# Down product of an encoder block: one more pair of k tiles by seven products in the second half of columns

## The chip, the cores and the metric

The kernel runs on one core of a Trainium2 chip. The metric is the device time of one execution in microseconds (us); the kernel before takes 1113.47 us, the median of 3 runs (1113.41 to 1113.65). Engines are named as in the profile: PE (TensorE, the matmuls), PEld (its weight loads), DVE (VectorE), ACT (ScalarE), POOL (GpSimd) and SP (SyncE, here only an issuer of DMAs).

## The reference, cut to what matters

One encoder block over 256 positions of width 2048: a mixer, then a gated conv-MLP, then a per-layer embedding gate. The change lies in the MLP, whose inner width is 5632:

```python
def conv_glu(hn, w_up, conv_w, conv_b, w_down):
    up = hn @ w_up
    gate, val = jnp.split(up, 2, axis=-1)
    gate = dwconv_centred(gate, conv_w, conv_b)
    return (jax.nn.gelu(gate, approximate=True) * val) @ w_down
```

All of it is float32. The last line's product, (256 x 5632) by (5632 x 2048), is called the down product here; `hn @ w_up` is up, and the gate product of the embedding that follows is (256 x 2048) by (2048 x 2048).

## The kernel before

**Arithmetic.** PE multiplies numbers of the shortened type fp32r, so each float32 operand is split in a high part (a cast on ACT, L153 for weights, L945 for activations) and a low part (a subtraction on DVE, L154 and L946). One product becomes three: high by high, high by low, low by high.

**The down product** runs in two halves of 1024 columns, `dn0` and `dn1` (`sublayer`, L835, and `token_major`, L306). In each half the 44 k tiles of 128 rows are taken as 22 pairs, u = 0 to 21; pair u has the tiles k = 2u and 2u + 1, and tiles in traces bear the number k: `dn122` is the second half's pair u = 11. A pair is done in one of two ways.

- *Ordinary*: the pair's weights (128 x 2048 values, 1 MB, tile `dn1r`) are loaded and split in two parts of 1024 (`dn_0`, `dn_1`); PE does 24 matmuls of 512 columns (2 k tiles, 2 halves of the tokens, 2 halves of the columns, 3 products).
- *By seven products* (`seven_products`, L256): the pair is read as a 2 x 2 matrix of blocks by a 2 x 2 matrix of blocks, and Strassen's scheme in Winograd's form needs 7 block products in place of 8, so 21 matmuls of 512. It needs sums of blocks on both sides. On the weight side the sums s1 to s4 are four DVE additions of 128 x 512 (`add_blocks`, L250); they are made while up runs and are kept in DRAM, so that a pair loads two blocks of the weights themselves (tile `r`, 768 KB) and the page with the sums (tile `t`, 1 MB). These are split in four parts, named a (512 wide), b, d and c (1024 wide each), in this order. On the activation side the sums are 128 x 512 values with their low parts (tile `hd`, 512 KB): for some pairs (`dn_stored`) they are made while up runs and are stored in `hsum` (L955 to L965), and POOL's queue loads them (L1073); for the others DVE and ACT make them on the spot (L803 to L808). The partial products that belong to several outputs are collected in four accumulators (`dns`, `dn0s`, `dn1s`) over all the pairs so treated, and `combine` (L284) adds them up once per half.

`dn_fast` (L920) lists the pairs by seven products: 17 in the first half, 15 in the second. Ordinary in the second half are u = 0, 1, 6, 10, 17, 20 and 21. At u = 11 of the second half the job `first` loads and splits a first piece of the gate product's weights (`gtf`, 1 MB).

**Up** runs in 176 pieces of 16 matmuls. Between the pieces other jobs are set out by a hand-written list, `jobs_at`: for each pair in `which` (the pairs of the down and the gate product by seven products, 37 of them, two of which come last) a `fetch` of the weights at piece n, and at piece n + 3 an `add` (the four additions) and a `store` to DRAM on POOL's queue (tile `dns`); the last two stay in SBUF. In up the order within ACT, DVE and SP is the order of the program (`in_order`, L200). In down a scheduler at build time decides the order on each engine; on the chip each engine takes its instructions in that fixed order.

**Buffers** that decide when something can start: high parts and low parts of weights have 5 buffers each, raw weights 3 (so a load is issued when DVE has made the low part b of the pair that was loaded three loads before), activation parts `hs` 2, `mid` tiles (among them `hd`) 3, and pages of 128 x 2048 (weight sums `t`, hidden activations, the gate weights) 13 in all. Loads of `r` and `t` are issued on SP's queue, loads of `hd` on POOL's.

Of the kernel before, what the change touches and what calls it, by code (L numbers as in the profile page):

```python
# [53 lines left out]
def build(nc, a, out):  # L54
# [6 lines left out]
    with tile.TileContext(nc) as tc, \  # L61
# [165 lines left out]
        def block_sums(name, w, c0, k, held):  # L227


            pg = []  # L230

            def fetch():
                r = page(f"{name}b{c0}_{k}")
                pg.append(r)
                load(r, w[c0 // 1024, k // 2])

            def add():
                add_blocks(pg[0])
                if held:
                    sums_[name, c0, k] = pg[0], True  # L240

            def store():
                if not held:
                    t = dp.tile([P, 2048], F32, tag=f"{name}s{c0}_{k}", bufs=1, name=f"{name}s{c0}_{k}")
                    nc.gpsimd.dma_start(t, pg[0])  # L245
                    sums_[name, c0, k] = t, False

            return fetch, add, store
# [668 lines left out]
            h_kept.append(dp.tile([P, D], F32, tag=f"h{t}", bufs=1, name=f"h_kept{t}"))  # L917
        pl_kept = dp.tile([P, D], F32, tag="pl", bufs=1, name="pl_kept")

        dn_fast, gt_fast = ((2, 3, 4, 5, 7, 8, 9, 10, 11, 12, 13, 14, 15, 16, 17, 18, 19), (2, 3, 4, 5, 7, 8, 9, 11, 12, 13, 14, 15, 16, 18, 19)), ((4, 5, 6), (1, 2))  # L920

        dn_stored = (2, 3, 5, 7, 8, 10, 11, 13, 14, 16, 17, 18, 19)
        gt_ks = list(range(NK)), [0, 1, 8, 9, 10, 11, 2, 3, 4, 5, 6, 7, 12, 13, 14, 15]
# [6 lines left out]
        jobs_at[6].append(lambda: load(pl_kept, pl[0]))  # L930
        for i, w_ in enumerate(which[2:] + which[:2]):
            fetch, add, store = block_sums(*w_, i >= len(which) - 2)
            n = 46 * i // 10 + 4
            jobs_at[n].append(fetch)
            jobs_at[n + 3].extend((add, store))
        hid, kept = [], {}
# [87 lines left out]
        with in_order():  # L1024
            for _ in range(5):
                next_part()
            for n in range(NPIECES):
                s, v, i = blocks[n // 4]
# [235 lines left out]
```

## Time and profile before

| | |
|---|---|
| median of the runs | 1113.47 us |
| the profiled execution | 1113.6 us, its span 1111.8 us |
| granted PE clock, mean | 0.998 of full |
| up, from the first of its matmuls to the last | about 292 to 786 us of the span |
| down, first half and second half | about 786 to 896 us and 896 to 1007 us |

The span is what the profiler sees of one execution on the core; some 1.8 us of the measured time lie outside it. A view by windows gives the busy time of each engine in a stretch; a timeline lists instructions with their start and duration; the chain of waits goes back from the last instruction to what released it. Busy times on DVE and ACT are of single instructions that overlap at their ends: how fast an engine gets through a row of them is read from start to start.

### The profile page before, as it was taken

To read this page: it belongs to the slowest core of one execution; us is meant where nothing else is said; L and a number is where in the kernel's file an instruction comes from. 1 tells how busy PE (TensorE), PEld (TensorE's weight loads), DVE (VectorE), ACT (ScalarE), POOL (GpSimd) and SP (SyncE) were. 2 spreads that over 40 slices of the span, in tenths; PEclk is the share of its full clock that TensorE was granted. 3 is DMA by queue.
4 is the path that set the end of the run, shared out by engine and by line. 5 is a ranking of instruction groups with operands and counts; after the bars stand their busy time and mean duration, and the time that the engine had idled before them with its cause. 6 is when DMAs were issued, how large, how long until landed. Compare 5 with 4: busy or idle time off the path is not lost.

```text
span 1111.8 us, 16068 instructions
## 1 busy us (share of the span) xinstructions
PE 1102.2 (99%) x5964; PEld 951.3 (86%) x5964; DVE 959.5 (86%) x1339; ACT 724.0 (65%) x1057; POOL 75.7 (7%) x140
## 2 busy tenths in 40 slices
PE   9999999999999999999999999999999999999997
PEld 9999988888888888888888888888888888888876
DVE  6568997899868998888888888898899999999995
ACT  6958763555775564665655646657579877877673
POOL 0200000100100000000000000000000000021001
PEclk9999999999999999999999999999999999999999
DMA  9853356454589999999899999899999899996763
GB/s 363 323 195 140 114 188 267 152 190 171 194 357 401 401 372 385 350 377 374 341 378 374 360 383 366 351 392 390 353 384 386 333 344 399 413 394 226 274 237 105
DMA packets 54943, 347.29 MB, mean 312 GB/s; under 512 B 6096, under 2 KB 6992, under 8 KB 20176
## 3 DMA queue, kind: packets, MB, share of 16 engines
q1 hardware_dynamic: 44064, 289.53, 67.1%
q0 software_dynamic: 10368, 56.10, 13.4%
q8 instruction: 47, 0.77, 0.3%
q10 hardware_dynamic: 432, 0.62, 0.2%
q14 instruction: 32, 0.26, 0.1%
HBM read 297.48 MB, written 48.76 MB: 311 GB/s over the span
## 4 chain that ended last, share of the span: by engine, by line
PE 92%; ACT 3%; DMA 2%; DVE 1%; issue 1%; POOL 0%; SPq 0%; POOLq 0%; ACTq 0%
PE ga L90 22%; PE va L90 22%; PE dna L90 12%; PE woa L90 7%; PE xbc L90 5%; PE gt L90 5%; PE z L90 4%; PE dns L90 4%; PE dn0s L90 2%; PE dn1s L90 2%; DMA dtur<-w_dtu 2%; PE ple L90 1%; DMA x<-x 1%; PE yd L90 1%; PE pw L90 1%
## 5 line engine op out<-in xcount | busy, mean ns | idle before, releaser
L90 PE MATMUL ga<-wox,ug_0h 128*128 128x512 f32 x352 | 125.5, 395 | 0.0
L90 PE MATMUL ga<-wox,ug_1h 128*128 128x512 f32 x352 | 125.1, 394 | 0.0
L90 PE MATMUL va<-wox,uv_1h 128*128 128x512 f32 x352 | 124.8, 393 | 0.0
L90 PE MATMUL va<-wox,uv_0h 128*128 128x512 f32 x352 | 124.8, 393 | 0.0
L90 PE MATMUL ga<-wox,ug_1l 128*128 128x256 f32 x352 | 99.1, 282 | 0.0
L90 PE MATMUL va<-wox,uv_1l 128*128 128x256 f32 x352 | 99.1, 281 | 0.0
L90 PE MATMUL va<-wox,uv_0l 128*128 128x256 f32 x352 | 99.1, 281 | 0.0
L90 PE MATMUL ga<-wox,ug_0l 128*128 128x256 f32 x352 | 99.0, 281 | 0.0
L254 DVE TENSOR_TENSOR dnb<-dnb 128x512 f32<-128x512 f32 x128 | 88.3, 690 | 3.1
L90 PEld LDWEIGHTS va<-wox,uv_0h 128*128 128x128 f32 x352 | 66.1, 188 | 15.0
L90 PEld LDWEIGHTS va<-wox,uv_1h 128*128 128x128 f32 x352 | 66.1, 188 | 15.0
L90 PEld LDWEIGHTS ga<-wox,ug_1h 128*128 128x128 f32 x352 | 66.1, 188 | 15.0
L90 PEld LDWEIGHTS ga<-wox,ug_0h 128*128 128x128 f32 x352 | 66.1, 188 | 14.8
L90 PEld LDWEIGHTS ga<-wox,ug_0l 128*128 128x128 f32 x352 | 66.2, 188 | 0.1
L90 PEld LDWEIGHTS ga<-wox,ug_1l 128*128 128x128 f32 x352 | 66.2, 188 | 0.0
L90 PEld LDWEIGHTS va<-wox,uv_1l 128*128 128x128 f32 x352 | 66.2, 188 | 0.0
L90 PEld LDWEIGHTS va<-wox,uv_0l 128*128 128x128 f32 x352 | 66.2, 188 | 0.0
L945 ACT CAST hs<-hid 128x512 fp32r<-128x512 f32 x44 | 27.1, 620 | 17.7 <-PE dna L90 17.6
L245 POOL DMA_DIRECT2D dns<-dnb x30 | 16.2, 540 | 309.9 <-DVE dnb L254 299.9
L946 DVE TENSOR_TENSOR hs<-hid,hs 128x512 fp32r<-128x512 f32 x44 | 30.0, 688 | 3.4 <-ACT hs L945 3.4
L807 ACT CAST he<-he 128x512 fp32r<-128x512 f32 x13 | 8.1, 621 | 36.6 <-DVE he L806 36.6
L90 PE MATMUL dna<-dn_0h,hs 128*128 128x512 f32 x96 | 31.3, 394 | 0.0
(2247 smaller groups left out, 3235.5 us busy)
## 6 DMA issues: line engine op xcount, KB each, us to landing
dnb<-w_down SPq DMA_DIRECT2D x32, 1024.0 KB, 10.0
dns<-dnb POOLq DMA_DIRECT2D x30, 1024.0 KB, 6.7
hd<-hsum POOLq DMA_DIRECT2D x24, 512.0 KB, 8.5
zr<-w_z SPq DMA_DIRECT2D x8, 1024.0 KB, 5.0
dtur<-w_dtu SPq DMA_DIRECT2D x14, 528.0 KB, 8.2
wo0r<-w_out_ SPq DMA_DIRECT2D x7, 1024.0 KB, 4.8
dn1r<-w_down SPq DMA_DIRECT2D x7, 1024.0 KB, 9.2
hsum<-he POOLq DMA_DIRECT2D x13, 512.0 KB, 7.1
```

The lines of the kernel that those rows point to most:

```text
L90: last["pe"] = ins(nc.tensor.matmul(o, lhsT, rhs, start=start, stop=stop, skip_group_check=True))
L245: nc.gpsimd.dma_start(t, pg[0])
L254: nc.vector.tensor_add(v[:, i], v[:, i], v[:, j])
L807: nc.scalar.copy(o[:, :512], s[:, :512])
L945: nc.scalar.copy(t[:, :512], hid_part(k))
L946: nc.vector.tensor_sub(t[:, 512:], hid_part(k), t[:, :512].bitcast(F32))
```

## The change

The pair u = 10 (k tiles 20 and 21) of the second half of columns is moved from the ordinary pairs to those by seven products. Its activation sums are already made and stored for the first half (10 is in `dn_stored`), and its weight sums join the list of blocks in up, which then has 38 entries; the factor that spreads the entries over the pieces of up goes from 46 to 45 tenths.

```diff
-        dn_fast, gt_fast = ((2, 3, 4, 5, 7, 8, 9, 10, 11, 12, 13, 14, 15, 16, 17, 18, 19), (2, 3, 4, 5, 7, 8, 9, 11, 12, 13, 14, 15, 16, 18, 19)), ((4, 5, 6), (1, 2))
+        dn_fast, gt_fast = ((2, 3, 4, 5, 7, 8, 9, 10, 11, 12, 13, 14, 15, 16, 17, 18, 19), (2, 3, 4, 5, 7, 8, 9, 10, 11, 12, 13, 14, 15, 16, 18, 19)), ((4, 5, 6), (1, 2))
...
         for i, w_ in enumerate(which[2:] + which[:2]):
             fetch, add, store = block_sums(*w_, i >= len(which) - 2)
-            n = 46 * i // 10 + 4
+            n = 45 * i // 10 + 4
             jobs_at[n].append(fetch)
             jobs_at[n + 3].extend((add, store))
```

In the built program the second half then has 21 matmuls for this pair in place of 24, four weight splits on ACT and on DVE in place of two, a load of 768 KB and one of 1 MB on SP's queue in place of one of 1 MB, and one more load of 512 KB on POOL's queue; up has four more additions on DVE, one more 1 MB load and one more 1 MB store.

## The prediction

> **What bounds the kernel now.** I read the page first, then the chain of waits, then windows, then the timelines of DVE, PE, ACT and POOL around the pair that changes.
>
> ```profile
> span 1111.8 us, 16068 instructions
> PE 1102.2 (99%) x5964; PEld 951.3 (86%) x5964; DVE 959.5 (86%) x1339; ACT 724.0 (65%) x1057; POOL 75.7 (7%) x140
> PE 92%; ACT 3%; DMA 2%; DVE 1%; issue 1%; POOL 0%; SPq 0%; POOLq 0%; ACTq 0%
> ...
> 763.69 22.33 PE va L90 x128
> ...
> 500.00:550.00 50.00, 50.00 (x289) 43.90 (x288) 42.36 (x57) 31.03 (x47) 2.66 (x5) 1.00 0.92 357
> 896.00:1006.00 110.00, 110.00 (x478) 89.45 (x477) 104.64 (x128) 84.20 (x107) 12.01 (x11) 1.00 0.96 385
> 946.00:976.00 30.00, 30.00 (x132) 24.40 (x131) 29.93 (x38) 25.25 (x33) 2.15 (x4) 1.00 1.01 409
> ```
>
> The first rows (page) give PE as the bound of the whole: 99% busy, 92% of the chain that ended last. A window's columns are PE, PEld, DVE, ACT and POOL busy, granted PE clock, DMA share, GB/s. The three windows are a stretch of up, all of the second down half, and its 30 us from pair u = 11 on. In up DVE has some 15% to spare. In the last window nothing has: PE 30.00 of 30, DVE 29.93 of 30, the DMA engines at a share of 1.01. A cut of PE's work is worth its time there only if the other two still deliver in time. So the share of the span is the wrong view for this change; the question is by how much DVE and the DMAs are ahead of PE at u = 11 and after.
>
> **What PE saves.** The chain of waits shows PE's pieces in order (start, duration, engine, tile, count):
>
> ```profile
> 937.64 2.07 PE dna L90 x9
> 942.47 2.08 PE dna L90 x9
> 946.63 5.55 PE dna L90 x24
> 952.87 2.07 PE dna L90 x9
> ```
>
> From 942.47 back to 937.64 is 4.83 us: one pair by seven products, 21 matmuls. The ordinary pair u = 10 is the 24 matmuls from 946.63: 5.55 us, 0.231 us each. Three fewer save 3 x 0.231 = 0.69 us, all of it on the path. That is the whole gain that the change can have: 0.06% of the span.
>
> **What DVE gains in work.** The timeline of DVE around the pair (start, duration, engine, line, operation, tiles, count; idle time before and its releaser in brackets):
>
> ```profile
> 940.82 1.23 DVE L154 TENSOR_TENSOR dn118dl<-dn118t,dn118dh 128x1024 fp32r<-128x1024 f32 x1 [0.74 <-ACT dn118dh L153]
> ...
> 943.10 1.22 DVE L154 TENSOR_TENSOR dn_0l<-dn1r,dn_0h 128x1024 fp32r<-128x1024 f32 x1
> 944.24 1.22 DVE L154 TENSOR_TENSOR dn_1l<-dn1r,dn_1h 128x1024 fp32r<-128x1024 f32 x1
> ...
> 945.97 2.35 DVE L154 TENSOR_TENSOR gtfl<-gtf,gtfh 128x1024 fp32r<-128x1024 f32 x2
> ...
> 948.85 0.68 DVE L154 TENSOR_TENSOR dn122al<-dn122r,dn122ah 128x512 fp32r<-128x512 f32 x1
> 949.45 1.22 DVE L154 TENSOR_TENSOR dn122bl<-dn122r,dn122bh 128x1024 fp32r<-128x1024 f32 x1
> ...
> 952.24 1.22 DVE L154 TENSOR_TENSOR dn122dl<-dn122t,dn122dh 128x1024 fp32r<-128x1024 f32 x1
> ...
> 954.51 0.69 DVE L946 TENSOR_TENSOR hs<-hid,hs 128x512 fp32r<-128x512 f32 x1
> 955.12 0.69 DVE L154 TENSOR_TENSOR dn124al<-dn124r,dn124ah 128x512 fp32r<-128x512 f32 x1
> 955.72 1.22 DVE L154 TENSOR_TENSOR dn124bl<-dn124r,dn124bh 128x1024 fp32r<-128x1024 f32 x1
> 956.85 1.22 DVE L154 TENSOR_TENSOR dn124dl<-dn124t,dn124dh 128x1024 fp32r<-128x1024 f32 x1
> ...
> 985.12 1.22 DVE L154 TENSOR_TENSOR dn136cl<-dn136t,dn136ch 128x1024 fp32r<-128x1024 f32 x1 [0.52 <-ACT dn136ch L153]
> ```
>
> DVE waits before 940.82, and the next wait that the timeline marks is the one before 985.12: between them it runs back to back through u = 10 to 17. From start to start a split of 1024 takes 1.14 us (943.10 to 944.24) and one of 512 takes 0.60 (948.85 to 949.45). The ordinary pair's two splits cost 2 x 1.14 = 2.28. By seven products they are four: 0.60 + 3 x 1.14 = 4.02. DVE gets 1.74 us more, in a row without a hole, so everything that it delivers until 985 comes 1.74 us later. Ordinary pairs are the places where DVE draws ahead of PE (2.28 and the 0.60 of an L946 against 5.55 us), and u = 10 stands just before `gtf`, 2.35 us that belong to no pair. The edit takes away the rest that paid for it.
>
> **How far DVE is ahead.** PE's first uses of those parts, from its timeline:
>
> ```profile
> 952.02 0.39 PE L90 MATMUL dns<-dn122ah,hs 128*128 128x512 f32 x1
> 954.32 0.39 PE L90 MATMUL dna<-dn122dl,hs 128*128 128x512 f32 x1
> 957.78 0.40 PE L90 MATMUL dna<-dn124bl,hs 128*128 128x512 f32 x1
> 958.93 0.39 PE L90 MATMUL dna<-dn124dl,hs 128*128 128x512 f32 x1
> ```
>
> `dn122dl` is done at 952.24 + 1.22 = 953.46 and used at 954.32: 0.86 us ahead. `dn124bl` is done at 956.94, used at 957.78: 0.84. `dn124dl`: 958.07 against 958.93, 0.86. After the change DVE is 1.74 later, while PE asks 0.69 earlier.
>
> Step by step, with the order of the built program. For u = 11 it puts an L946 (0.60) ahead of `dn122dl`, and makes the matmul that needs `dn122dl` the 14th of the pair in place of its 11th. `dn122dl` is done at 953.46 + 1.74 + 0.60 = 955.80. PE would begin the pair at 952.02 - 0.69 = 951.33 and reach the 14th at 951.33 + 13 x 0.231 = 954.33. PE waits 1.47 us. It is then 1.47 - 0.69 = 0.78 later than before. `dn124bl` comes at 956.94 + 1.74 = 958.68 and is asked for at 957.78 + 0.78 = 958.56: 0.12 more. `dn124dl` comes at 959.81 and is asked for at 959.83: nothing. The short cut agrees: 1.74 of work less the smallest lead of 0.84 is 0.90. Behind the waiting matmul stand all later ones, since PE takes them in order; what is late next is nothing, because u = 17 (ordinary, not changed) again gives DVE time, and the idle before 985.12 shows that it then waits for others. What PE lost by then is not made up.
>
> **What the DMAs gain in work.** ACT's wait for a load, POOL's loads of activation sums, and the times to landing in the second half:
>
> ```profile
> 949.21 1.06 ACT L153 CAST dn122dh<-dn122t 128x1024 fp32r<-128x1024 f32 x1 [0.47 <-DMA dn122t<-dns]
> ...
> 937.24 0.54 POOL L1073 DMA_DIRECT2D hd<-hsum  x1 [14.69 <-DVE dn116dl L154]
> 946.93 0.54 POOL L1073 DMA_DIRECT2D hd<-hsum  x1 [9.15 <-PE dn1s L90]
> ...
> dn1r<-w_down SPq DMA_DIRECT2D x5, 1024.0 KB, 9.2
> hd<-hsum POOLq DMA_DIRECT2D x9, 512.0 KB, 8.4
> ...
> dn118t<-dns SPq DMA_DIRECT2D x1, 1024.0 KB, 10.9
> ...
> dn118r<-w_down SPq DMA_DIRECT2D x1, 768.0 KB, 8.8
> ```
>
> In place of one load like `dn1r` come one like `dn118r`, one like `dn118t` and one `hd`: 768 + 1024 + 512 - 1024 = 1280 KB more, 1.31 MB. The engines are full at 409 GB/s (window above), so all that lands behind it lands up to 1.31 / 0.409 = 3.2 us later. `dn122t` landed at 949.2, when ACT began; 3.2 later is 952.4, the cast `dn122dh` ends at 953.5, and DVE, busy with its own queue, wants it only at 955.80 - 1.22 = 954.58. So 1.1 us of cover is left, and the DMAs add nothing beyond DVE's delay. Bounds: 0, or the whole 3.2 in place of the 0.90 if that cover and the later ones fail. I take 0, nearest to the row with the wait of 0.47. On POOL's queue the new load takes the place of 937.24 and the next one moves to about 942, when u = 8 frees a `mid` buffer; landing 8.4 later, at 950.4, it is still ahead of its first use by the 7th matmul, 951.33 + 6 x 0.231 = 952.7.
>
> The Trainium skill, SBUF — State Buffer, section Summary: rules for kernel authors, tells one to reckon transfers between HBM and SBUF at about 358 GB/s. By that page the extra load would be an estimate of 3.7 us in place of 3.2; the trace differs, with 409 GB/s in the window, and the measurement decides.
>
> **ACT and up.** ACT gets two casts more there; it is busy 84.20 of 110 us in the second half, so its own waits for PE cover them. In up, one block more: four additions, one load, one store.
>
> ```profile
> L254 DVE TENSOR_TENSOR dnb<-dnb 128x512 f32<-128x512 f32 x128 | 88.3, 690 | 3.1
> ...
> 775.16 1.22 DVE L154 TENSOR_TENSOR uv_1l<-uv101r,uv_1h 128x1024 fp32r<-128x1024 f32 x1
> ...
> 783.31 0.28 PE L90 MATMUL va<-wox,uv_1l 128*128 128x256 f32 x1
> ```
>
> 4 x 0.69 = 2.8 us of DVE, spread with the others (45 tenths of a piece for 46). The last part of up is made at 776.38 and used at 783.31, 6.9 us ahead; PE's stretches of 128 matmuls have no hole (22.33 above). I take 0; with the cover gone it is 2.8.
>
> **The sum.** -0.69 (PE) + 1.47 + 0.12 (waits for DVE) + 0 (DMA) + 0 (ACT, up) = +0.90 on the profiled execution's 1113.6 us (span 1111.8 and 1.8 around it): 1114.5. The median shown is 0.1 lower, 1113.47, so I say 1114.4.
>
> **The rivals.**
> - *The saving arrives.* DVE is in time after all, for instance because its row before 985 can close up, and 0.69 comes off: 1112.8. For it: PE's three matmuls are certain. Against: leads of 0.84 to 0.86 against 1.74 of new work with no idle to take it.
> - *The DMAs become the bound (slower).* From u = 10 to 16 the stretch is paced by bytes and ends 3.2 later: 1113.6 + 3.2 = 1116.8. It decides once loads come over 1.1 us later than reckoned at `dn122t`. For it: share 1.01, and ACT already waits for `dn122t`. Against: DVE's own delay of 1.74 covers half. By the Trainium skill's rate above it would be 1117.3, an estimate.
> - *Up loses its cover.* The denser additions make PE wait there, up to 2.8 on top: 1117.3. Against: the lead of 6.9.
> - *The change does not do what it says.* Excluded by the built program: 21 matmuls stand in place of 24.
>
> **How the numbers follow.** Forecast 60% (its own range 1113.6 to 1116.0: PE waits from half to twice the reckoned 1.59), DMA-bound 23%, saving arrives 9%, up 6%, anything else 2%. A measurement of this kernel can tell about 0.2% from no change, 2.2 us: below 1111.2 is faster, above 1115.7 slower. Faster 0.02: no gain beyond 0.69 is to be had. Slower: 0.23 + 0.06 and 0.03 from the forecast's upper end, 0.32. Within: 0.66. The range leaves out the last part of either end: 1112.7 to 1117.0.
>
> **What would show it.** Right: PE waits of 1 to 2 us in all at u = 11 and 12 of the second half, for DVE's low parts; u = 10 in 4.83 us; up unchanged at 22.33 per 128; the end of down some 0.9 later. Wrong: no PE wait there, waits for a DMA at u = 11 to 16, or a hole in up's matmuls.

## The result and the profile after

| | before | after |
|---|---|---|
| median, same chip (22 runs each) | 1113.55 us (1113.03 to 1114.44) | 1115.12 us (1114.01 to 1117.05) |
| the profiled execution | 1113.6 us, span 1111.8 | 1116.33 us, span 1114.5 |

The ratio is 1.0015, with a 95% interval of 1.0009 to 1.0021: 1.6 us slower. The executions of after lie twice as far apart as those of before. The profiled one, 2.7 us slower than that of before, is among the slower, so its waits say where time is lost, and not how much the median execution loses at each place.

From the page of after (span; busy time of each engine; the chain that ended last by engine):

```profile
span 1114.5 us, 16077 instructions
...
PE 1102.9 (99%) x5961; PEld 950.5 (85%) x5961; DVE 964.2 (87%) x1345; ACT 725.3 (65%) x1059; POOL 72.1 (6%) x142
...
PE 90%; ACT 3%; DMA 2%; DVE 2%; issue 1%; POOL 0%; SPq 0%; POOLq 0%; ACTq 0%
```

By windows (a stretch of up, the second half of down, its 30 us from 946 on; columns as before):

```profile
500.00:550.00 50.00, 50.00 (x288) 43.90 (x287) 42.45 (x57) 31.78 (x48) 2.12 (x4) 1.00 0.98 373
896.00:1006.00 110.00, 108.25 (x466) 86.56 (x465) 104.32 (x129) 84.77 (x107) 7.18 (x12) 1.00 0.98 394
946.00:976.00 30.00, 29.44 (x125) 22.77 (x124) 29.93 (x36) 25.42 (x32) 2.15 (x4) 1.00 1.02 418
```

From the chain of waits, up's piece that answers to the one of before:

```profile
763.91 22.33 PE va L90 x128
```

The page's 99% for PE says nothing; the window does. PE, which was busy for the whole of the second half before, now lacks 1.75 us of its 110. Up's 128 matmuls take 22.33 us as before. The view of PE's waits in down's second half, which has no row before, has three:

```profile
PE dna L90 <- ACT hs L945: 1.2, 1, 1.2
PE dna L90 <- DVE dn122dl L154: 0.4, 1, 0.4
PE dns L90 <- ACT dn122ch L153: 0.2, 1, 0.2
```

PE's timeline at u = 10 and 11 (start, duration, line, tiles; idle time before and its releaser in brackets):

```profile
946.68 0.39 PE L90 MATMUL dns<-dn120ah,hs 128*128 128x512 f32 x1
...
951.51 0.40 PE L90 MATMUL dns<-dn122ah,hs 128*128 128x512 f32 x1
...
953.37 0.39 PE L90 MATMUL dna<-dn122bh,hd 128*128 128x512 f32 x1
953.68 0.50 PE L90 MATMUL dna<-dn122dh,hs 128*128 128x512 f32 x1
954.02 0.40 PE L90 MATMUL dn1s<-dn122dh,hd 128*128 128x512 f32 x1
954.62 0.50 PE L90 MATMUL dns<-dn122ch,hd 128*128 128x512 f32 x1 [0.21 <-ACT dn122ch L153]
954.97 0.39 PE L90 MATMUL dn1s<-dn122ch,hd 128*128 128x512 f32 x1
955.71 0.50 PE L90 MATMUL dna<-dn122dl,hs 128*128 128x512 f32 x1 [0.35 <-DVE dn122dl L154]
956.05 0.40 PE L90 MATMUL dna<-dn122dh,hs 128*128 128x512 f32 x1
```

The pair u = 10 takes 951.51 - 946.68 = 4.83 us: the three matmuls are saved. Starts that follow each other by more than 0.231 us are time lost, and that is more than the brackets say, since PE's step behind a wait is longer too (0.34 us from 955.71 to 956.05). From 953.37 to 954.97 four steps take 1.60 in place of 0.92, 0.68 lost to the high parts `dn122dh` and `dn122ch`; from there to 956.05 two take 1.08 in place of 0.46, 0.62 lost to the low part `dn122dl`. With 0.10 more at u = 12 the first wait is 1.40 us. The two rows that feed these matmuls, on ACT and on DVE:

```profile
952.57 1.05 ACT L153 CAST dn122dh<-dn122t 128x1024 fp32r<-128x1024 f32 x1 [1.36 <-DMA dn122t<-dns]
954.44 1.22 DVE L154 TENSOR_TENSOR dn122dl<-dn122t,dn122dh 128x1024 fp32r<-128x1024 f32 x1
```

ACT waited for the load of `dn122t`, so the high parts are late by the load; the low part, done at 955.66, is late by DVE's row. The second wait stands where the prediction has none, at the ordinary pair u = 17. PE's timeline first, then ACT's, then SP's queue with the issue of the load that ACT waited for (first in the kernel before, then in the change), and that load's row in the change's view of DMA issues (its last number is the time to landing):

```profile
981.77 0.39 PE L90 MATMUL dn1s<-dn132ch,hd 128*128 128x512 f32 x1
983.35 0.72 PE L90 MATMUL dna<-dn_0h,hs 128*128 128x512 f32 x2 [1.19 <-ACT hs L945]
```

```profile
977.02 1.05 ACT L153 CAST dn132dh<-dn132t 128x1024 fp32r<-128x1024 f32 x1 [1.39 <-DMA dn132t<-dns]
977.97 1.04 ACT L153 CAST dn132ch<-dn132t 128x1024 fp32r<-128x1024 f32 x1
980.78 1.05 ACT L153 CAST dn_0h<-dn1r 128x1024 fp32r<-128x1024 f32 x1 [1.77 <-PE dna L90]
981.74 1.04 ACT L153 CAST dn_1h<-dn1r 128x1024 fp32r<-128x1024 f32 x1
982.69 1.14 ACT L945 CAST hs<-hid 128x512 fp32r<-128x512 f32 x2
```

```profile
966.19 0.33 SPq L120 DMA_DIRECT2D dn1r<-w_down  x1
...
967.78 0.33 SPq L120 DMA_DIRECT2D dn1r<-w_down  x1
```

```profile
dn1r<-w_down SPq DMA_DIRECT2D x1, 1024.0 KB, 12.9
```

PE loses 983.35 - 981.77 - 0.23 = 1.35 us, and the profile names the activation cast `hs`. That cast is only the last of a row on ACT: it stands behind `dn_0h` and `dn_1h`, and `dn_0h` starts at 980.78. For that cast the profile names PE, but the load was issued at 967.78 and took 12.9: it landed at 980.7. The cause of PE's wait is thus a late load, two steps behind the name in the bracket. Before, it was issued 1.59 us earlier and took 9.6: it landed at 975.8, 4.9 us earlier. So 1.6 us of its lateness is later issue and 3.3 a longer way. The issue hangs on DVE: it follows the low part `dn128bl`, which frees a raw buffer and is done at 967.75 in place of 966.16. In all the profiled execution has -0.69 + 1.40 + 1.45 (0.10 for the longer step behind the wait at u = 17 included) = 2.16 us more at the end of this half; its start into down was 0.2 later from up on. That is more than the 1.57 us between the medians; how these divide between the two waits is not shown.

### The profile page after: what moved, and what is told of

The parts are those of the page before. It is cut to its first block, busy times and chain, and to the rows that moved or that the text cites. A ratio compares the mean times of both kernels' runs of the same rounds, so it can differ in the third digit from the quotient of the medians.

```text
span 1114.5 us, 16077 instructions
## 1 busy us (share of the span) xinstructions
PE 1102.9 (99%) x5961; PEld 950.5 (85%) x5961; DVE 964.2 (87%) x1345; ACT 725.3 (65%) x1059; POOL 72.1 (6%) x142
## 4 chain that ended last, share of the span: by engine, by line
PE 90%; ACT 3%; DMA 2%; DVE 2%; issue 1%; POOL 0%; SPq 0%; POOLq 0%; ACTq 0%
PE ga L90 22%; PE va L90 22%; PE dna L90 11%; PE woa L90 7%; PE xbc L90 5%; PE gt L90 5%; PE z L90 4%; PE dns L90 4%; PE dn0s L90 2%; DMA dtur<-w_dtu 2%; PE dn1s L90 2%; PE ple L90 1%; DMA x<-x 1%; PE yd L90 1%; PE pw L90 1%
## 5 line engine op out<-in xcount | busy, mean ns | idle before, releaser
L254 DVE TENSOR_TENSOR dnb<-dnb 128x512 f32<-128x512 f32 x132 | 91.1, 690 | 3.2
L946 DVE TENSOR_TENSOR hs<-hid,hs 128x512 fp32r<-128x512 f32 x44 | 29.9, 685 | 2.3 <-ACT hs L945 2.3
L90 PE MATMUL dna<-dn_0h,hs 128*128 128x512 f32 x88 | 29.0, 394 | 1.2 <-ACT hs L945 1.2
```

The lines of the kernel that those rows point to most:

```text
L90: last["pe"] = ins(nc.tensor.matmul(o, lhsT, rhs, start=start, stop=stop, skip_group_check=True))
L254: nc.vector.tensor_add(v[:, i], v[:, i], v[:, j])
L946: nc.vector.tensor_sub(t[:, 512:], hid_part(k), t[:, :512].bitcast(F32))
```

## The experiments

The theories as they stood: DVE's row (A), the loads (B), or both (M, later T) make PE wait; a fourth, C, blames up. Each run was timed beside the kernel before on the same chip, 11 executions each (the kernel before 15 to 33); given are the medians and, behind them, the difference to before.

**Up alone.**

```diff
-            n = 46 * i // 10 + 4
+            n = 45 * i // 10 + 4
```

> The kernel before with the spacing of up's block sums alone (45 tenths in place of 46; no 38th entry, no more pair by seven products). Theory M (the late DVE row at u = 11 and 12 costs some 0.7 us net, late loads at u = 17 the rest): nothing of the loss comes from up, so the time is that of before, 1113.5 us within 0.3. Rival C (the new spacing, or what it does to up's loads, costs part of it): 1114.0 or more. If the time is that of before, the loss sits in down's second half.

1113.52 us, ratio 1.0000 (0.9992 to 1.0009). No cost of the new spacing is to be seen. The 38th entry was not run by itself, but up in the profile of after has no hole either.

**Less for DVE at u = 10.** The pair's matmuls use the low part of c for b and d too.

```diff
...
-            b2 = split(f"{name}b", r[:, 1024:], 1024)
+            b2 = split(f"{name}b", r[:, 1024:], 1024, low=not extra)
...
-            t42 = split(f"{name}d", t[:, 1024:], 1024)
+            t42 = split(f"{name}d", t[:, 1024:], 1024, low=not extra)
+            if extra:
+                b2, t42 = (b2[0], t31[1]), (t42[0], t31[1])
```

> The changed kernel, in which the pair u = 10 of the second half leaves out two of its subtractions for low parts (b and d, 1024 columns each, 2 x 1.14 = 2.28 us of DVE's row); its matmuls take the low part of c in their place, so that the products of that pair are not the reference's. Loads, casts and matmuls stay. Theory M: the wait for dn122dl at u = 11 shrinks to what the landing of dn122t leaves of it (cast from 952.6, low part done about 954.8 against 954.5 asked, so 0.3 or less), and the wait at u = 17 stays, since its loads are as late as before: 1115.1 - 1.0 = 1114.1 us, 1113.8 to 1114.5. Rival A (DVE's row alone costs the time; the wait at u = 17 comes from DVE running late too): both waits go, 1112.8. Rival B (the loads alone set both waits): 1115.1, no change.

1114.96 us, +1.45, ratio 1.0014 (1.0005 to 1.0023): as slow as the change. The order on ACT and on both DMA queues is the same as in the change. DVE's timeline in this run:

```profile
944.61 0.69 DVE L950 TENSOR_TENSOR hs<-hid,hs 128x512 fp32r<-128x512 f32 x1 [0.77 <-ACT hs L949]
946.68 1.23 DVE L155 TENSOR_TENSOR dn120cl<-dn120t,dn120ch 128x1024 fp32r<-128x1024 f32 x1 [1.37 <-ACT dn120ch L153]
947.82 2.35 DVE L155 TENSOR_TENSOR gtfl<-gtf,gtfh 128x1024 fp32r<-128x1024 f32 x2
```

and ACT's:

```profile
952.70 1.06 ACT L153 CAST dn122dh<-dn122t 128x1024 fp32r<-128x1024 f32 x1 [1.65 <-DMA dn122t<-dns]
953.66 1.05 ACT L153 CAST dn122ch<-dn122t 128x1024 fp32r<-128x1024 f32 x1
```

DVE hands 0.77 + 1.37 = 2.14 of its 2.28 us straight back, waiting for casts: its row is fed by ACT's row, which is no shorter. So this run takes little of DVE's delay away (`dn122dl` starts at 954.09 in place of 954.44), and its median can't say what DVE's delay costs. And the page `dn122t` lands as late as before (cast from 952.70), so that PE still loses 1.0 us at u = 11, 0.8 of it to the high parts (0.7 before DVE's relief), and 1.06 at u = 17. There the profile now names the load itself:

```profile
980.05 1.05 ACT L153 CAST dn_0h<-dn1r 128x1024 fp32r<-128x1024 f32 x1 [1.60 <-DMA dn1r<-w_down]
```

A (DVE's row alone) does not fit these rows, and neither does the share of M that gave DVE all of the wait at u = 11: most of what is left there is a wait for the load. By number the run fits B, but that says little, since the relief did not arrive.

**Fewer bytes at u = 10.** One raw load in place of three loads.

```diff
-            if (stage, c0, k0) in sums_:
+            if (stage, c0, k0) in sums_ and not extra:
...
+            if k == 20 and cur["d"][0] == 16:
+                d = cur["d"][1]
...
```

> The changed kernel, in which the pair u = 10 of the second half loads neither its page of block sums nor its activation sums: it splits the raw tile of 1 MB twice and takes the activation sums of u = 8, so that its products are not the reference's. The bytes are those of an ordinary pair (1.31 MB fewer than the change, 3.2 us at 410 GB/s), DVE's and PE's instructions are those of the change. Theory M: the wait at u = 17 goes (its weights land some 3 us earlier), the wait for DVE's low part at u = 11 stays at about 1 us: 1115.1 - 1.3 = 1113.8 us, 1113.5 to 1114.2. Rival A (DVE's row alone): 1115.1, no change. Rival B (the loads alone set both waits): 1112.8.

1113.65 us, +0.14, ratio 1.0003 (0.9994 to 1.0012). The time lies in M's range and 0.85 us above B's, but the waits are not where M puts them, and it is not a clean test: with other loads the scheduler also set ACT's and DVE's instructions in another order (one half of `gtf`'s split comes ahead of `dn120dh`, and four additions of activation sums no longer stand ahead of `dn122dl`). What it does show is that PE can do u = 11 to 13 with no wait and the pair's three matmuls saved; smaller waits, of 0.46 and 0.58 us, come at u = 15 and 17. At u = 17 the load of the weights, issued at 966.20, still took 12.4 us, with 1.31 MB fewer asked for at u = 10: why, the runs do not show.

**gtf behind u = 17.** `first` at 18 in place of 11.

```diff
-                      fast=dn_fast, sums=hid_sums, at={11: first, NF // 2: lambda: (ple_parts(), back())}, row=rf, ...)
+                      fast=dn_fast, sums=hid_sums, at={18: first, NF // 2: lambda: (ple_parts(), back())}, row=rf, ...)
```

> The changed kernel with the load, two casts and two subtractions for the first gate pair moved from ahead of u = 11 to ahead of u = 18, which is behind the loads and splits of the ordinary pair u = 17. Down's rows are relieved of 2.28 us of DVE, 2 casts and 1 MB of loads between u = 11 and u = 17. Theory M: both waits go; where the moved work itself costs nothing at u = 18 and 19, 1112.8 us (all of the 0.69 us of PE arrives). Rival A (DVE alone): the same. Rival B (bytes alone; the load is only moved to a place where the loads are as dense): the waits appear at u = 19 or at gate's start, 1114 to 1115.

1116.01 us, +2.5, ratio 1.0021 (1.0012 to 1.0030). In its profile both waits are gone, and the matmuls from u = 11 to the start of u = 18 run 0.73 us ahead of before, counted from the start of the half: all of the saving. Then, at the end of down, PE's waits read:

```profile
PE dna L90 <- DVE dna L304: 0.6, 1, 0.6
PE dnxt L395 <- DVE hb L864: 0.3, 1, 0.3
PE dns L90 <- ACT dn136ch L153: 0.2, 1, 0.2
```

The longest is for DVE's last additions to the accumulators (L304), at 1003.5. `gtf`'s subtractions ended 20 us before it, at 982.5, and DVE waited 1.86 and 0.37 us for casts in between, so the profile does not tie this wait to them; the order on PE and DVE at the end of down is another one too. No theory gave +2.5. The profiled execution (1114.2) is the fastest of the eleven; what makes the others 1 to 3 us slower is not in a trace.

**Half of the page t, and both reliefs.** The pair loads half its page and splits that half twice; in the second kernel DVE's two low parts are left out as well.

```diff
+                    h0 = 1024 if (stage, c0, k0) == ("dn", 1024, 20) else 0
-                    last["dma"] = load(t, sums_[stage, c0, k0][0], True)
+                    last["dma"] = load(t[:, h0:], sums_[stage, c0, k0][0][:, h0:], True)
...
-            t31 = split(f"{name}c", t[:, :1024], 1024)
+            t31 = split(f"{name}c", t[:, h0:h0 + 1024], 1024)
```

> The changed kernel, in which the pair u = 10 of the second half loads only the second 1024 columns of its page of block sums (0.5 MB fewer, 1.28 us at 410 GB/s) and splits them twice, so that its products are not the reference's. Work and order on ACT and DVE are those of the change up to u = 13. Theory T, formed after the run with fewer subtractions: at u = 11 the loads (dn122t, then two casts on ACT) and DVE's row are late by about the same, so that either alone keeps the wait; at u = 17 the loads alone are late. Then DVE's row still holds PE at u = 11 (low part done at about 955.7 as in the change), and the wait at u = 17 loses 1.2 of its 1.35 us: 1113.9 us, 1113.5 to 1114.3. Rival B (the loads alone set both waits): both nearly go, 1112.9 to 1113.2. Rival A (DVE's row alone): 1115.1.

> The changed kernel with both reliefs at u = 10 of the second half: half the page of block sums is loaded (0.5 MB fewer), and the low parts of b and d are left out (2.28 us of DVE's row fewer); the products of that pair are not the reference's. Theory T (two limits at u = 11, the loads at u = 17): both waits go but for 0.2 to 0.4 us: 1112.9 to 1113.3, and less than with half the page alone by 0.7 or more. Rival B (the loads alone): 1112.9 to 1113.2, and the same as with half the page alone within 0.3. If a wait of over 0.7 us stays at u = 11, a third limit (ACT's row of casts) holds it: 1113.6 or more.

1114.95 us (+1.6, ratio 1.0018, 1.0009 to 1.0027) and 1114.85 us (+1.5, ratio 1.0012, 1.0003 to 1.0020): no gain. T and B said otherwise for both; A's time for the first, 1115.1, is met, and so is the condition that the second names for a third limit, but the profiles show that the loads were not relieved. SP's queue in the first of the two, then ACT in the second:

```profile
944.38 0.33 SPq L120 DMA_DIRECT2D dn126r<-w_down  x1
944.76 0.51 SPq L120 DMA_DIRECT2D dn122t<-dns  x1
```

```profile
954.63 1.04 ACT L153 CAST dn122dh<-dn122t 128x1024 fp32r<-128x1024 f32 x1 [2.96 <-DMA dn122t<-dns]
```

With the shorter load the scheduler put `dn126r` ahead of `dn122t` on SP's queue. `dn126r` has to wait for a raw buffer, and `dn122t` is issued behind it at 944.76, where the change issues it at 940.71. So it lands no earlier (4.1 us later issue, 7.4 in place of 11.8 us to landing). The first kernel's profiled execution, 1113.95 us, is its fastest: it has 1.4 us of wait at u = 11, for the casts behind the late load and not for DVE, and none at u = 17; the other ten are slower. So these two runs do not test the theories; they show that a late `dn122t` holds PE at u = 11 with DVE relieved (1.35 us in the second, put down to the cast `dn122dh`).

**gtf's load early.** A load moved to a place where the DMA engines have room, so that nothing is left out and the loads at u = 10 stay as they are.

```diff
-            r, hi, lo = page("gtf"), page("gtfh", F32R), page("gtfl", F32R)
-            last["dma"] = load(r, w_gate[0, 0])
+            r, hi, lo = cur.pop("gtf"), page("gtfh", F32R), page("gtfl", F32R)
...
+        def fetch_first():
+            cur["gtf"] = page("gtf")
+            last["dma"] = load(cur["gtf"], w_gate[0, 0])
...
-                      at={11: first, ...
+                      at={1: fetch_first, 11: first, ...
```

> The changed kernel, in which only the load for the first gate pair (gtf, 1 MB) is issued ahead of u = 1 of the second half, where the profile shows the DMA engines at a share of 0.75 to 0.85 (866 to 896 us); its casts and subtractions stay ahead of u = 11. From u = 11 on the loads come 1 MB, 2.6 us at 410 GB/s, earlier; DVE's work is that of the change, in another order around u = 11. Theory T: the wait at u = 17 goes, and at u = 11 DVE's row leaves 0.5 to 1.2 us: 1113.3 to 1114.0. Rival B (the loads alone): 1112.8 to 1113.0, faster than before by the 0.69 us of the matmuls. Rival A (DVE alone): 1115.1.

1114.40 us, +1.06, ratio 1.0009 (1.0000 to 1.0018): 0.4 us above T's range, 0.7 below A's time and 1.4 above B's. `dn122t`, which now takes `gtf`'s place on SP's queue, is issued at 936.07 in place of 940.71. ACT's timeline has no wait for a load before `dn136dh` at 983, and all that PE waits for is DVE. PE's waits in the second half, by the view of waits:

```profile
PE dna L90 <- DVE dn126dl L154: 0.2, 1, 0.2
PE dna L90 <- DVE dn128bl L154: 0.2, 1, 0.2
```

With the short slips beside them (0.40 at u = 12, 0.50 at 13, 0.45 at 14, by starts as above) PE loses 1.35 us in the profiled execution. All of it is at low parts, and the wait at u = 17 is gone: the load of its weights is issued even later than in the change, at 968.29, but takes 8.6 us in place of 12.9. So the loads account for the second wait, and with them out of the way DVE's row makes the kernel some 1 us slower than before. The place differs from the forecast's (u = 12 to 14, not 11), since the built order around u = 11 is another one.

**The same with two subtractions fewer** (the edit of the second experiment on top):

> The changed kernel with gtf loaded ahead of u = 1 (its splits at u = 11), and the low parts of b and d at u = 10 left out (2.28 us of DVE; that pair's products are not the reference's). With the loads out of the way DVE's work alone is halved again. Theory T: the 1.0 to 1.1 us that the kernel with the early load is slower than before comes from DVE's row, so it goes; the cast hd again stands ahead of dn126dh and costs up to 0.5: 1112.8 to 1113.3. Rival (DVE's row has no part in it): 1114.4, no change from the early load alone.

1113.69 us, +0.18, ratio 1.0000 (0.9991 to 1.0009). The time is 0.4 us above T's range and 0.7 below the rival's. Against the early load alone it is 1.06 - 0.18 = 0.9 us less. The two intervals overlap, and DVE's and PE's orders differ besides the two subtractions; but the profiles agree: from u = 5 to u = 18 the early load alone falls 0.70 us behind before and this kernel gains 0.15, and its only wait of over 0.1 us is for a cast (0.35 at u = 13), none for a low part.

**All of gtf early**: its splits too, at u = 6, 5 and 8 in place of 11.

```diff
-                      at={1: fetch_first, 11: first, ...
+                      at={1: fetch_first, 6: first, ...
```

> As the kernel before this one, and the two casts and two subtractions of gtf come ahead of the ordinary pair u = 6 in place of u = 11: 2.28 us of DVE and 1 MB of loads leave the stretch from u = 10 to u = 17. Theories T and B: both waits go, 1112.8 us, if DVE has that time at u = 6 to 9, where before waits 0.74 us and more for buffers; if it has not, the wait is moved there, 1113.5 or more. Rival A (DVE alone): 1112.8 too. It is the version that could be faster than the kernel before.

> The changed kernel with gtf loaded ahead of u = 1 of the second half and cast and subtracted ahead of u = 5. In the built order the cast of the activation sums that PE lets go late (hd, in the run with gtf at u = 6 ahead of dn126dh, where ACT waited 0.99 us for PE and PE then 0.6 us for dn126ch) stands behind dn126ch. Theory T: with the loads, DVE's row and this cast out of the way no wait is left from u = 11 to 17, and the 0.69 us of the three matmuls arrives: 1112.7 to 1112.9. If DVE has no 2.28 us to spare at u = 5 to 9, a wait appears there: 1113.5 or more. Rival D (the time is set by something that none of the moves touches): 1113.4, as with gtf at u = 6.

> As the kernel before this one, with gtf's casts and subtractions ahead of u = 8. Theory T: 1112.7 to 1113.0 if the 2.28 us of DVE fit between u = 8 and u = 10; DVE's row is then full from u = 8 on, and what it lacks appears as a wait at u = 11 to 13, at most the 1.0 us that lay between the load alone early and all of gtf early. Rival D: 1113.4.

1113.37 us (+0.03, 0.9992 to 1.0010), 1113.48 us (-0.03, 0.9992 to 1.0009) and 1113.20 us (-0.31, 0.9990 to 1.0007). The kernel then computes all that the change computes, and the slowdown is gone. The 0.69 us of the matmuls are not shown in any of the three medians: all three intervals take in no change, the first two lie at rival D's 1113.4, and the last between D and T. D, a limit that none of the moves touches, is thus not excluded for the whole time. At u = 6 the timelines of ACT and PE show a part of the loss, 0.59 us:

```profile
961.47 0.62 ACT L807 CAST hd<-hs 128x512 fp32r<-128x512 f32 x1 [0.99 <-PE dn1s L90]
962.00 1.04 ACT L153 CAST dn126dh<-dn126t 128x1024 fp32r<-128x1024 f32 x1
962.95 1.04 ACT L153 CAST dn126ch<-dn126t 128x1024 fp32r<-128x1024 f32 x1
```

and PE's, at u = 13:

```profile
964.04 0.51 PE L90 MATMUL dns<-dn126ch,hd 128*128 128x512 f32 x1 [0.22 <-ACT dn126ch L153]
```

A cast of activation sums waits for PE to let go of a buffer, and the casts that PE itself needs stand behind it. In the built order for u = 5 and u = 8 it stands behind them. With u = 8 the 30 us window and the whole half have PE full:

```profile
896.00:1006.00 110.00, 110.00 (x478) 89.28 (x477) 106.66 (x132) 86.01 (x110) 15.18 (x15) 1.00 0.98 400
946.00:976.00 30.00, 30.00 (x131) 24.19 (x130) 29.87 (x39) 25.02 (x32) 2.15 (x4) 1.00 1.02 418
```

Its span is 1111.0 us, 0.8 less than before's, but 0.60 of that was there when down began; from u = 5 to u = 18 PE is 0.54 us faster than before. Its executions go from 1112.77 to 1114.63 us, and the median difference is within what can be told from none. DVE and the DMAs are still full (29.87 of 30, 1.02).

**The control**: the same move in the kernel before.

> The kernel before (u = 10 an ordinary pair, 46 tenths) with the same move of gtf alone: its load ahead of u = 1, its casts and subtractions ahead of u = 8. PE has no wait in the second half before, so there is nothing that the move could take away. Theory T: the time is that of before, 1113.4 us within 0.3, and the 0.5 us by which the run with the pair and this move was shorter from u = 4 to u = 18 are the pair's three matmuls. Rival: the move itself brings it, 1113.0 or less.

1113.45 us, -0.02, ratio 0.9999 (0.9990 to 1.0008). The move alone brings nothing, and in its profile PE's time from u = 5 to u = 18 is that of before within 0.03 us, so the 0.54 us that PE gains in the profile with u = 8 are the pair's.

## Why the prediction was right, and where it was not

- *PE saves 0.69.* Right: 4.83 us for u = 10, and the two profiles without a wait at u = 11 to 13 (fewer bytes, and gtf behind u = 17) begin u = 14 0.70 and 0.72 us ahead of before.
- *DVE is late at u = 11, 1.47 + 0.12.* Right in kind, in place and nearly in size: `dn122dl` starts at 954.44 and ends at 955.66 against 955.80 reckoned, PE's 14th matmul of the pair starts at 955.71, and the first wait is 1.40 in place of 1.59. Part of that agreement is luck. The L946 that the sum adds (0.60) fell into the idle time ahead of `dn118dl`; in its place came a start 0.22 later and 0.23 of waiting ahead of `dn120dl`. And 0.68 of the 1.40 is a wait for the high parts, which the sum does not have; had they been there, PE would have asked for `dn122dl` at 951.51 + 13 x 0.231 = 954.51 and waited 1.15 for DVE. With the loads out of the way the net is +1.06 us (gtf's load early) against +0.90 in the sum, in another order and with the waits at u = 12 to 14.
- *The DMAs add nothing beyond DVE's delay.* This is the step that failed. The landing was reckoned well: 952.4, and ACT's cast started at 952.57. But it was held only against DVE, which wants the cast at 954.58, and called 1.1 us of cover. PE itself asks for the high parts `dn122dh` and `dn122ch`, as its 10th and 12th matmul, and loses 0.68 us to them before it comes to the low part. So at u = 11 DVE's lateness and the load's lie on top of each other: with low parts in time, PE would still have lost 0.7 to 0.8 us there, as the run with fewer subtractions shows. That run's median hardly moved for this reason and because DVE got only 0.14 of its 2.28 us; with the load early the same edit went with 0.9 us.
- *What is late next is nothing, because u = 17 again gives DVE time.* Wrong. It gives DVE time, but what is late at u = 17 is its own load: issued 1.6 us later behind DVE's row, 12.9 us to landing in place of 9.6, and 1.45 us of PE in the profiled execution. Behind u = 10 all loads came late: those of 1 MB issued between 940 and 968 us took 8.6 to 11.5 us before and 11.8 to 15.7 after, about the 3.2 us more that the prediction reckoned for 1.31 MB. Between the medians, each against its own before, the early load is worth 1.57 - 1.06 = 0.5 us; the intervals of the two overlap, so the size is an estimate. It is the term put at 0, and it would be most of the 0.7 us by which the forecast is low. The time fell in the range because the term that was missed is small beside the range.
- *The DMA-bound rival* put the deciding point at loads 1.1 us later than reckoned at `dn122t`. They came as reckoned there, and the loads cost time all the same. Its price, 3.2, did not come: at u = 17 the load landed 4.9 us later than before, but before it had landed 5.3 us ahead of PE's first use (981.06), and PE came to it 0.94 us later than before even without that wait, so that it lost 1.45 us.
- *ACT and up at 0.* Up: right. ACT has no place in the sum, and it was not harmless: its casts are the step between load and DVE, and one that waits for PE holds back others behind it.

## What to carry to other kernels

Where PE, DVE and the DMAs are all full, an edit that takes work from the one and gives more to the two others is paid for out of their lead; reckon for each pair that follows when PE itself, not only the next engine, asks for each thing, and follow the bytes to the next pair that needs a load of its own. A relief that brings nothing does not clear its resource: look first whether it arrived at all, and remember that two limits at one place hide each other, and have to be taken away one by one and together. Where a scheduler decides the order, compare the order of the variant before its time is read.

## What the runs showed of the hardware

- The change's executions spread wider: the kernel before stays within 1.4 us over 22 of them, the change within 3.0. That DVE and the DMAs are full does not settle it: with `gtf`'s load early, where they are as full, 11 executions lie within 1.0. In the two kernels that load half a page, with the same order on SP's queue, `dn122t` was issued at 944.76 and 944.91 and landed 7.4 us later in the one and 9.6 in the other. Why landing times differ between executions was not settled.
- With more loads waiting, the window of 30 us moved 418 GB/s after and 409 before. The Trainium skill, HBM Reference, section Specifications (TRN2), states about 425 GB/s for a core that streams alone; the two windows agree with it, 2 to 4% below.
- A bracket names the engine that came last by the profile, not the cause: the 1.77 us ahead of `dn_0h` are put down to PE, where the load landed at that moment.
